# Moving the weight parts of a two-block transformer kernel by 64 bytes within the on-chip memory

## Chip, cores, metric

The kernel runs on one core of a Trainium2 chip. The metric is the device time of one execution, in microseconds (us). It runs a whole small network: a hybrid block of two layers, the second of them with a mixture of experts, and a second block of two layers with attention. All of it is in float32, for one sequence of 256 tokens of width 1024.

## The reference, cut to what matters

```python
def swiglu(h, w1, w3, w2):
    a = jnp.einsum("btd,df->btf", h, w1)
    g = jnp.einsum("btd,df->btf", h, w3)
    return jnp.einsum("btf,fd->btd", jax.nn.silu(a) * g, w2)      # d 1024, f 2816

def moe_swiglu(h, w_router, w1, w3, w2):                          # 8 experts, top 2
    ...
    for e in range(N_EXPERTS):
        out = out + combine[..., e:e + 1] * swiglu(h, w1[e], w3[e], w2[e])
    return out

def reference(...):
    x = first_block(...)     # 2 layers: mixer (h @ w_in ... @ w_out), then swiglu or moe_swiglu
    return second_block(...) # 2 layers: attention (h @ w_in ... @ w_out), then swiglu
```

Around each of these eight steps there are norms, a modulation (shift, scale and gate from a vector `c`) and a residual sum.

## The kernel before

**Exact parts.** A product of float32 numbers is made of three fast matmuls. Each operand is split into a high part and a low part, and `mm3` (lines 166 to 168) adds high times high, high times low and low times high into the same accumulator in PSUM. The activations' parts are made where the activations are made. The weights come from memory as blocks of 1 MB into a buffer `raw` (in the experts also `rawx`), and `split_now` makes two halves of each block into parts: ScalarE copies 128x1024 numbers, rounded, into a tile `hi` (line 147), and VectorE subtracts that from the block into a tile `lo` (line 148). TensorE then reads `hi` and `lo`.

**Moving and stationary.** `matmul(out, lhsT=..., rhs=...)` loads `lhsT` into the array (a row PEld in the profile) and streams `rhs` through it. A profile's group name gives the moving operand first: `pp<-h,hi` streams the activations `h` through the weights `hi`, and `pp<-hi,xe` streams the weights `hi` through the activations `xe`.

**The stages**, in order of time: a mixer (44 to 175 us), a dense feed-forward (198 to 383), the second mixer (383 to 541), the router (541 to 589), eight experts (589 to 1384), attention (1407 to 1546), feed-forward (1570 to 1753), attention (1753 to 1893), feed-forward (1915 to 2100).

- A **feed-forward** goes in 11 steps of 256 hidden columns. From the second step on, `proj_tr` streams `h` (256 columns) through the weights: 2 matrices x 2 halves x 8 x 3 = 96 matmuls. Then `down` (line 634) streams 512 columns of the weights w2 through the hidden activations, which lie in scratch tiles `s`: 24 matmuls. In the first step the roles in the projection are the other way round (`pp<-hi,h`).
- An **expert** goes in five blocks of 512 hidden columns and one of 256. Weights are moving, the gathered tokens stationary; these tokens lie in scratch tiles `xe` for experts 0, 1, 4 and 5, and in the tiles `h` and `x` for experts 2, 3, 6 and 7. The product with w2 streams weights through scratch tiles `s` into `ya`.
- **Mixer and attention** use `proj_nat` for most products: weights moving, `h` stationary, 256 wide (`pj<-hi,h`). Their output product is 512 wide, with weights moving.

**Where tiles lie.** Each pool of tiles takes one piece of every partition of the on-chip memory, the pools behind one another in the order in which they are opened. `__init__` opens const, raw, hi, lo, x, h, t, macc, gate, col; the scratch pools of each step (`xe`, `s`, `y`, `rawx` and others) are opened later and lie behind these. Tiles of raw, x and h have 8192 bytes per partition, those of hi, lo, macc and gate 4096; the 32 tiles of t take 4096 bytes in all, the ten of col 320. So in the kernel before, the start addresses in a partition are these (the same slice steps of 512 bytes and more are used inside all of them):

| tiles | first address, bytes | remainder by 256 |
|---|---|---|
| raw | 24736 | 160 |
| hi | 57504 | 160 |
| lo | 82080 | 160 |
| x | 106656 | 160 |
| h | 131232 | 160 |
| macc | 151712 | 160 |
| first scratch tiles (f, xe, sh) | 168416 | 224 |
| s of 2048 bytes, y, rawx | 172512, 214496, 209376 | 224 |

Some scratch tiles of the two mixers have the remainder 32, since a pool with tiles of 1036 bytes lies ahead of them.

Of the kernel before, what the change touches and what calls it, by code (L numbers as in the profile page):

```python
# [20 lines left out]
KD = 8  # L21
# [38 lines left out]
# the second block's attention, in units of four heads: Q queries and keys, V values, A attention, F modulation  # L60
# [3 lines left out]
class _Net:  # L64
    def __init__(self, ctx, tc, a, out):
        self.tc, self.nc, self.a, self.out = tc, tc.nc, a, out
        self.pools = {}
        self.ctx = ctx
        for name, bufs in (("const", 1), ("raw", 4), ("hi", 6), ("lo", 6), ("x", 3), ("h", 1),
                           ("t", 32), ("macc", 2), ("gate", 2), ("col", 10)):  # L70
            self.pools[name] = ctx.enter_context(tc.tile_pool(name=name, bufs=bufs))
        self.n = 0
        self.bar, self.free = None, 0
        self.step = self.nraw = 0
# [11 lines left out]
    @contextmanager  # L86
    def phase(self, **sizes):
        """Scratch pools of one part of the program."""
        saved = dict(self.pools)
        with ExitStack() as st:  # L90
            for name, bufs in sizes.items():
                kw = {"space": PSUM} if name in ("pp", "pa", "ya", "pj", "sa", "sb", "sd") else {}
                self.pools[name] = st.enter_context(self.tc.tile_pool(name=name, bufs=bufs, **kw))
            yield
        self.pools = saved
# [26 lines left out]
    @contextmanager  # L122
    def behind(self):
        """Vector work that is issued behind the last normalisation's short steps."""
        ins = self.bar
        if ins is None or not any(i is ins for i in self.nc.cur_bb.bb.instructions):
            yield
            return
        with self.tc.issue_after(ins):
            yield  # L130
# [8 lines left out]
    def split_now(self, v):  # L139
        """Exact high and low parts of a [128, k, n] block: two lists of k tiles."""  # L140
        k, n = v.shape[1], v.shape[2]
        H, L = [], []
        for z in range(0, k, k // 2):
            m = k // 2
            h = self.tl("hi", [128, 1024], F32R)[:, :m * n].rearrange("p (k n) -> p k n", k=m)
            l = self.tl("lo", [128, 1024], F32R)[:, :m * n].rearrange("p (k n) -> p k n", k=m)
            self.nc.scalar.copy(h, v[:, z:z + m])  # L147
            self.nc.vector.tensor_tensor(l, v[:, z:z + m], h.bitcast(F32), ALU.subtract)  # L148
            H += [h[:, j] for j in range(m)]
            L += [l[:, j] for j in range(m)]  # L150
        return H, L
# [7 lines left out]
    def mm3(self, out, a, b, start, stop):  # L159
        """out += a^T b, a and b given as exact (high, low) parts."""  # L160
        mm = self.nc.tensor.matmul
        if b[1] is None:
            for i in range(2):
                mm(out, lhsT=a[i].bitcast(F32), rhs=b[0], start=start and i == 0, stop=stop and i == 1)
            return
        mm(out, lhsT=a[0], rhs=b[0], start=start, stop=False)  # L166
        mm(out, lhsT=a[0], rhs=b[1], start=False, stop=False)  # L167
        mm(out, lhsT=a[1], rhs=b[0], start=False, stop=stop)  # L168
# [9 lines left out]
    def rsqrt(self, v, n):  # L178
        """1/sqrt of v (> 0) to float32 accuracy."""
# [17 lines left out]
    def evac_split(self, ps, hi, lo, A=None, B=None):  # L197
        """ps [128, 2, n] in PSUM -> exact parts of ps * A + B (columns per middle index)."""
# [30 lines left out]
    def fill(self, n):  # L229
        """n more blocks of two rows of 128 of the modulation's product, behind the rest."""  # L230
# [15 lines left out]
    def plus(self, key, out, in_):  # L246
        """A gate row: the first layers add 1 to it."""
        if key[0] < 2:
            self.nc.scalar.activation(out, in_, ACT.Identity, bias=self.ones[:, 0:1])
        else:  # L250
            self.nc.scalar.copy(out, in_)

    def mod_gate_pe(self, key):
        """A gate on every partition, straight from the tensor engine, one half of the columns after the other."""
# [19 lines left out]
    def mod_rows(self, key):  # L274
        """Two rows of 128 into the sums by partition."""
# [20 lines left out]
    def mod_done(self, key):  # L296
        """The finished vector: a gate on every partition, shift and scale (plus 1) as columns."""
# [13 lines left out]
        if self.step in (2, 6):  # L311
            # the tensor engine is the busy one there: transposes, summed by the scalar engine
# [22 lines left out]
    def setup(self):  # L335
# [26 lines left out]
        def stack(tag, names, eng):  # L362
            """Vectors of 128-multiples, all as columns of one tile."""
# [58 lines left out]
    def rows(self, ap, n):  # L422
        """A row vector of n numbers, the same on every partition."""
        t = self.sc([128, n])
        self.nc.gpsimd.dma_start(out=t, in_=ap.partition_broadcast(128))
        return t

# [8 lines left out]
    def layer_norm(self, x):  # L436
        """x normalised (no gain, no bias), mostly on the scalar engine."""
# [19 lines left out]
    def affine(self, x, g, b):  # L457
        """x * g + b in place, with rows g and b from DRAM."""
# [12 lines left out]
    def make_hf(self, xn, A, B):  # L471
        """h^T = (xn * A + B)^T, [128, KD, T]."""
# [13 lines left out]
    def make_h(self, xn, A, B):  # L486
        """h^T = (xn * A + B)^T as exact parts, [128, KD, T]."""
# [21 lines left out]
    def ab(self, l, s, g=None, b=None):  # L509
        """Columns A = g (1 + scale), B = b (1 + scale) + shift."""  # L510
# [13 lines left out]
    def resid(self, get, x, gate, ln, norm=True):  # L524
        """xr = x (ALPHA with ln) + gate * y, y from get(t, h); xr and its rows normalised."""
# [43 lines left out]
    def resid_rms(self, get, x, gate, gb):  # L569
        """As resid with a layer norm (gain and bias rows in gb), then rows normalised by their mean square."""  # L570
# [34 lines left out]
    def proj_nat(self, h, w, c0):  # L605
        """h @ w[:, c0:c0+256], tokens on partitions: PSUM [128, 2, 256]."""
# [13 lines left out]
    def down(self, accs, blocks, t=None):  # L620
        """accs[t][h] += y^T W over blocks of 128 rows: (y parts, W parts, start, stop)."""
# [15 lines left out]
    def proj_out(self, accs, w, parts, last):  # L637
        """accs = y w over parts of 256 rows (row block, exact parts of y^T); token tiles apart in the last ones."""
# [17 lines left out]
    def ffn(self, h, w1, w3, w2, fill):  # L656
# [10 lines left out]
        for i in range(nstep):  # L667
            pss = []
            if i == 0:
                # tokens on partitions, so that the first tile can go ahead  # L670
# [38 lines left out]
    def mixer(self, l, h, fill):  # L709
# [10 lines left out]
        # small operands  # L720
# [12 lines left out]
        # dt, latents of the attention  # L733
# [10 lines left out]
        # xs, bm, cm with channels on partitions; causal convolution and silu  # L744
# [22 lines left out]
        # softplus  # L767
# [14 lines left out]
        # a, cumulative sums, decays  # L782
# [17 lines left out]
        # x with tokens on partitions  # L800
# [18 lines left out]
        # C B^T within the chunks  # L819
# [8 lines left out]
        for c in range(2):  # L828
            yp = self.ps(pool="sd")
            for g in range(2):  # L830
                # exp of the summed a from s to l, 0 where l < s
# [23 lines left out]
        # latent attention  # L855
# [57 lines left out]
        # what the output product takes, all parts  # L913
# [21 lines left out]
        # spatial gating  # L935
# [39 lines left out]
        # gate of the scan, twice silu(z); then normalised  # L975
# [36 lines left out]
    def scores(self, qT, kT, pool="pa"):  # L1012
        """Masked scores of one head, [128, 384]: (q0 k0), (q1 k0), (q1 k1)."""
# [6 lines left out]
    def softmax(self, p, scale, scol, sm):  # L1020
        """exp(scale (s - max)) and its sums; scale a number or columns by token tile."""
# [24 lines left out]
    def route(self, xn, hf):  # L1046
# [37 lines left out]
        # exact parts of xn  # L1084
# [4 lines left out]
        # sums over the experts stay in PSUM  # L1089
# [14 lines left out]
    def moe_over(self, st, A, B):  # L1104
        """Ranks from 128 on, for any expert with more than 128 tokens."""
# [5 lines left out]
    def granules(self):  # L1111
        """The experts' weights in the order of their use."""
# [18 lines left out]
    def expert_in(self, base, es, pos, gate, xh, xl, A, B):  # L1131
        """One-hot slots, gathered inputs (exact parts) and gates by slot for two experts, in pieces."""
# [122 lines left out]
    def rope_setup(self):  # L1255
        """cos and sin of position * frequency for any position, by exact reduction."""
# [14 lines left out]
        def rnd(dst, src, unit):  # L1271
            """src rounded to a multiple of unit, divided by unit."""
            V.tensor_scalar(dst, src, 1.0 / unit, MAGIC, ALU.mult, ALU.add)
            V.tensor_scalar(dst, dst, MAGIC, None, ALU.subtract)
# [33 lines left out]
        # back into [-pi, pi]  # L1308
# [15 lines left out]
    def tables(self, l):  # L1324
        nc, a = self.nc, self.a
        S, V = nc.scalar, nc.vector
        # rotation tables with the gains of q and k: [128, (q k), t, 16]
# [23 lines left out]
    def attn2(self, l, h):  # L1351
# [8 lines left out]
        def project(u):  # L1360
# [19 lines left out]
            # scale of the scores by query, [128, h, t]  # L1380
            scol = self.sc([128, 4, 2])
            V.tensor_scalar(scol, rs[:, 0:8].rearrange("p (t h) -> p h t", t=2), 0.125, None, ALU.mult)
            # rotation
# [104 lines left out]
    def run(self):  # L1488
# [8 lines left out]
        # which vectors of the modulation are worked out behind each step, how far behind, and in what portions  # L1497
# [105 lines left out]
```

## Time and profile before

| | |
|---|---|
| three runs | 2097.38, 2099.36, 2099.42 us |
| median | 2099.36 us |
| span of the profiled execution | 2100.0 us |
| TensorE busy in it | 1959.5 us, 93% of the span |
| VectorE busy | 1658.0 us, 79% |
| ScalarE busy | 1208.3 us, 58% |
| read from memory | 552.19 MB, 263 GB/s over the span |

The profiled execution has no time other than its span, which is 0.6 us above the median of the runs; a sum made against the span is carried over to the median by that difference. TensorE's busy time must be read with care: matmuls overlap, each row's duration reaches from a matmul's start to its modelled end, and so a row with 283 ns can stand for matmuls that start 120 ns after each other.

### The profile page before, as it was taken

To read this page: it belongs to the slowest core of one execution; us is meant where nothing else is said; L and a number is where in the kernel's file an instruction comes from. 1 tells how busy PE (TensorE), PEld (TensorE's weight loads), DVE (VectorE), ACT (ScalarE), POOL (GpSimd) and SP (SyncE) were. 2 spreads that over 40 slices of the span, in tenths; PEclk is the share of its full clock that TensorE was granted. 3 is DMA by queue.
4 is the path that set the end of the run, shared out by engine and by line. 5 is a ranking of instruction groups with operands and counts; after the bars stand their busy time and mean duration, and the time that the engine had idled before them with its cause. 6 is when DMAs were issued, how large, how long until landed. Compare 5 with 4: busy or idle time off the path is not lost.

```text
span 2100.0 us, 30041 instructions
## 1 busy us (share of the span) xinstructions
PE 1959.5 (93%) x11481; PEld 1681.4 (80%) x11481; DVE 1658.0 (79%) x2512; ACT 1208.3 (58%) x1817; POOL 50.1 (2%) x98
## 2 busy tenths in 40 slices
PE   3998999898599999999999999969989999998999
PEld 3887999886478787878778887858869998978998
DVE  6888977897588888888888888889778877667554
ACT  3454444452378767767776777755454446545442
POOL 4000000100000000000000000000000000000000
PEclk9999999998599999999999999979999999999999
DMA  9585998565489999899989999958339894326662
GB/s 319 181 287 202 339 331 308 177 224 204 141 300 360 328 339 334 317 358 346 340 322 348 344 360 351 360 181 278 124 132 346 322 320 147 121 87 214 203 199 80
DMA packets 283238, 555.25 MB, mean 264 GB/s; under 512 B 10172, under 2 KB 137520, under 8 KB 283088
## 3 DMA queue, kind: packets, MB, share of 16 engines
q1 hardware_dynamic: 280000, 549.49, 74.6%
q0 software_dynamic: 2656, 3.20, 0.8%
q8 instruction: 91, 1.49, 0.3%
q10 hardware_dynamic: 432, 0.58, 0.1%
q14 instruction: 59, 0.48, 0.1%
HBM read 552.19 MB, written 1.05 MB: 263 GB/s over the span
## 4 chain that ended last, share of the span: by engine, by line
PE 64%; DVE 5%; ACT 2%; issue 1%; DMA 1%; ACTq 0%; DVEq 0%
PE pp L167 12%; PE pp L168 11%; PE pp L166 11%; PE pa L634 6%; PE ya L167 4%; PE ya L166 4%; PE ya L168 4%; PE pp L175 3%; PE pj L166 1%; PE pj L167 1%; PE pj L168 1%; PE pp L171 1%; DVE lo L148 1%; PE sa L171 1%; ACT hi L147 1%
## 5 line engine op out<-in xcount | busy, mean ns | idle before, releaser
L148 DVE TENSOR_TENSOR lo<-raw,hi 128x1024 fp32r<-128x1024 f32 x660 | 787.5, 1220 | 193.1 <-ACT hi L147 191.5
L147 ACT CAST hi<-raw 128x1024 fp32r<-128x1024 f32 x660 | 668.4, 1051 | 393.6 <-PE pp L167 157.9
L166 PE MATMUL pp<-h,hi 128*128 128x256 f32 x960 | 274.4, 286 | 0.0
L168 PE MATMUL pp<-h,lo 128*128 128x256 f32 x960 | 271.6, 283 | 0.0
L167 PE MATMUL pp<-h,hi 128*128 128x256 f32 x960 | 271.5, 283 | 0.0
L148 DVE TENSOR_TENSOR lo<-rawx,hi 128x1024 fp32r<-128x1024 f32 x176 | 208.5, 1220 | 42.4 <-ACT hi L147 42.3
L294 DVE SCALAR_TENSOR_TENSOR macc<-raw,const,macc 128x1024 f32<-128x1024 f32 x168 | 215.3, 1281 | 6.6 <-DMA raw<-in_ada_w_dram 2.3
L167 PEld LDWEIGHTS pp<-h,hi 128*128 128x128 f32 x960 | 184.1, 192 | 1.9 <-issue 1.2
L166 PEld LDWEIGHTS pp<-h,hi 128*128 128x128 f32 x960 | 184.0, 192 | 1.8 <-ACT hi L147 1.0
L168 PEld LDWEIGHTS pp<-h,lo 128*128 128x128 f32 x960 | 184.1, 192 | 0.0
L147 ACT CAST hi<-rawx 128x1024 fp32r<-128x1024 f32 x176 | 176.5, 1048 | 11.9 <-PE pp L168 9.9
L166 PE MATMUL pj<-hi,h 128*128 128x256 f32 x576 | 169.6, 295 | 8.2 <-ACT h L505 3.7
L167 PE MATMUL pp<-lo,h 128*128 128x512 f32 (+1 forms) x480 | 174.6, 364 | 1.2 <-DVE lo L148 1.0
L166 PE MATMUL pp<-hi,h 128*128 128x512 f32 (+1 forms) x480 | 173.0, 361 | 0.0
L167 PE MATMUL pj<-lo,h 128*128 128x256 f32 x576 | 166.0, 290 | 0.8 <-DVE lo L148 0.8
L168 PE MATMUL pj<-hi,h 128*128 128x256 f32 x576 | 165.9, 290 | 0.0
L634 PE MATMUL pa<-hi,s 128*128 128x512 f32 x528 | 151.5, 396 | 0.0
L167 PE MATMUL pp<-lo,xe 128*128 128x512 f32 (+1 forms) x384 | 146.5, 382 | 1.3 <-DVE lo L148 1.0
L166 PE MATMUL pp<-hi,xe 128*128 128x512 f32 (+1 forms) x384 | 145.2, 379 | 0.0
L168 PE MATMUL pp<-hi,xe 128*128 128x512 f32 (+1 forms) x384 | 144.7, 377 | 0.0
L168 PE MATMUL pp<-hi,x 128*128 128x512 f32 (+1 forms) x384 | 143.2, 373 | 0.0
L167 PE MATMUL ya<-lo,s 128*128 128x512 f32 x352 | 141.9, 403 | 0.0
(481 smaller groups left out, 3563.3 us busy)
## 6 DMA issues: line engine op xcount, KB each, us to landing
raw<-in_moe_w_dram SPq DMA_DIRECT2D x176, 1024.0 KB, 6.1
rawx<-in_moe_w_dram SPq DMA_DIRECT2D x88, 1024.0 KB, 6.5
raw<-in_ada_w_dram SPq DMA_DIRECT2D x48, 1024.0 KB, 6.9
raw<-in_w_mod_dram SPq DMA_DIRECT2D x48, 1024.0 KB, 6.3
raw<-in_w_in_dram SPq DMA_DIRECT2D x42, 1024.0 KB, 5.8
raw<-in_ffn_w_dram SPq DMA_DIRECT2D x33, 1024.0 KB, 6.1
raw<-in_w_gate_dram SPq DMA_DIRECT2D x22, 1024.0 KB, 5.4
raw<-in_w_up_dram SPq DMA_DIRECT2D x22, 1024.0 KB, 5.5
```

Of the source, the lines that this page charges most:

```text
L147: self.nc.scalar.copy(h, v[:, z:z + m])
L148: self.nc.vector.tensor_tensor(l, v[:, z:z + m], h.bitcast(F32), ALU.subtract)
L166: mm(out, lhsT=a[0], rhs=b[0], start=start, stop=False)
L167: mm(out, lhsT=a[0], rhs=b[1], start=False, stop=False)
L168: mm(out, lhsT=a[1], rhs=b[0], start=False, stop=stop)
L171: self.nc.tensor.matmul(out, lhsT=lhsT, rhs=rhs, start=start, stop=stop)
L175: self.nc.tensor.transpose(out, in_, self.ident[:p, :p])
L294: V.scalar_tensor_tensor(acc, v[:, i], c, acc, ALU.mult, ALU.add)
L634: mm(accs[t][h], lhsT=y[ia][:, s], rhs=W[ib][:, h * 512:(h + 1) * 512], start=start and ia == 0 and ib == 0, stop=stop and ia == 1)
```

## The change

One tile of 64 bytes per partition is placed ahead of the pool hi, and one of 192 bytes ahead of the pool x. GpSimd fills both with zeros at the start. Nothing reads them. All tiles of hi and lo so move up by 64 bytes, and all tiles of x and of the pools behind x by 256 bytes.

```diff
         self.ctx = ctx
+        self.pads = []
         for name, bufs in (("const", 1), ("raw", 4), ("hi", 6), ("lo", 6), ("x", 3), ("h", 1),
                            ("t", 32), ("macc", 2), ("gate", 2), ("col", 10)):
+            if name in ("hi", "x"):
+
+                pad = ctx.enter_context(tc.tile_pool(name=f"pad{name}", bufs=1))
+                n = 16 if name == "hi" else 48
+                self.pads.append(pad.tile([128, n], F32, name=f"pad{name}", tag="pad"))
             self.pools[name] = ctx.enter_context(tc.tile_pool(name=name, bufs=bufs))
+        for p in self.pads:
+            tc.nc.gpsimd.memset(p, 0.0)
```

The other lines of the diff drop comments and docstrings; a line number after the change is 8 higher. By the remainder by 256, the tiles stand like this:

| tiles | before | after |
|---|---|---|
| raw | 160 | 160 |
| hi, lo (the weights' parts) | 160 | 224 |
| x, h, macc | 160 | 160 |
| xe, s, y, rawx (scratch) | 224 | 224 |

The order of the instructions and what each waits for is the same on TensorE, VectorE, ScalarE and SyncE. GpSimd has two more, at the start of its program. Before, from its first row on (the names are constants and the first mixer's tiles):

```order
5 L1599 UNCONDITIONAL_BRANCH
6 L353 MEMSET const_105 128x128
7 L355 MEMSET const_107 128x128
8 L402 MEMSET const_274 128x384
9 L753 MEMSET cx_573 128x3
```

And with the change:

```order
5 L1607 UNCONDITIONAL_BRANCH
6 L79 MEMSET padhi 128x16
7 L79 MEMSET padx 128x48
8 L361 MEMSET const_115 128x128
9 L363 MEMSET const_117 128x128
10 L410 MEMSET const_284 128x384
11 L761 MEMSET cx_583 128x3
```

The two rows of the pads now stand ahead of the constants, and all that follows on GpSimd is two short instructions later.

## Rows read from the trace of the kernel before

**Rows 1.** Head of the page: the profiled execution.
```profile
span 2100.0 us, 30041 instructions
```

**Rows 2.** Windows by stage; the columns stand in the first line.
```profile
core 0: us, PE busy (x) PEld busy (x) DVE busy (x) ACT busy (x) POOL busy (x), PEclk, DMA share, GB/s
...
383.00:541.00 158.00, 128.99 (x813) 112.39 (x812) 140.34 (x293) 70.66 (x147) 10.58 (x21) 0.86 0.63 214
...
589.00:1384.00 795.00, 784.21 (x3686) 634.16 (x3684) 679.54 (x664) 578.42 (x671) 2.68 (x5) 1.00 0.96 342
...
1570.00:1753.00 183.00, 182.15 (x1261) 168.47 (x1261) 139.84 (x137) 86.03 (x153) 5.43 (x8) 1.00 0.86 305
...
1915.00:2100.00 185.00, 179.28 (x1235) 165.78 (x1233) 96.96 (x95) 73.37 (x81) 0.00 (x0) 1.00 0.53 177
...
600.00:690.00 90.00, 90.00 (x437) 74.07 (x436) 83.00 (x83) 72.66 (x84) 0.00 (x0) 1.00 0.99 359
```

**Rows 3.** Chain that ended last, 1915 to 2100 us: start, us, what.
```profile
1928.30 5.60 PE pa L634 x24
1945.40 5.60 PE pa L634 x24
```

**Rows 4.** PE groups by form, whole run; last figure ahead of the bar: mean ns.
```profile
L167 PE MATMUL pp<-h,hi 128*128 128x256 f32 x960 | 271.5, 283 | 0.0
...
L168 PE MATMUL pj<-hi,h 128*128 128x256 f32 x576 | 165.9, 290 | 0.0
L634 PE MATMUL pa<-hi,s 128*128 128x512 f32 x528 | 151.5, 396 | 0.0
...
L168 PE MATMUL ya<-hi,s 128*128 128x512 f32 x352 | 139.3, 396 | 0.0
...
L634 PE MATMUL pa<-lo,s 128*128 128x512 f32 x264 | 85.0, 396 | 0.0
```

**Rows 5.** PE groups by form, experts only, 600 to 1380 us.
```profile
L166 PE MATMUL pp<-hi,h 128*128 128x512 f32 x320 | 125.5, 393 | 0.0
L168 PE MATMUL pp<-hi,x 128*128 128x512 f32 x320 | 125.2, 391 | 0.0
...
L166 PE MATMUL pp<-hi,xe 128*128 128x512 f32 x291 | 115.4, 397 | 0.0
L168 PE MATMUL pp<-hi,xe 128*128 128x512 f32 x292 | 115.3, 395 | 0.0
...
L168 PE MATMUL pp<-hi,x 128*128 128x256 f32 x64 | 18.1, 283 | 0.0
L166 PE MATMUL pp<-hi,h 128*128 128x256 f32 x64 | 18.1, 283 | 0.0
...
L166 PE MATMUL pp<-hi,xe 128*128 128x256 f32 x64 | 17.7, 277 | 0.0
L168 PE MATMUL pp<-hi,xe 128*128 128x256 f32 x64 | 17.7, 276 | 0.0
L171 PE MATMUL pa<-s,s 128*128 128x512 f32 x56 | 17.1, 400 | 0.2
L171 PE MATMUL pp<-s,x 128*128 128x256 f32 x48 | 11.8, 279 | 0.0
```

**Rows 6.** DVE and ACT groups by form, experts only, 600 to 1380 us.
```profile
L148 DVE TENSOR_TENSOR lo<-raw,hi 128x1024 fp32r<-128x1024 f32 x339 | 398.2, 1219 | 45.6 <-ACT hi L147 44.8 <-PE pp L168 0.2
L148 DVE TENSOR_TENSOR lo<-rawx,hi 128x1024 fp32r<-128x1024 f32 x172 | 203.6, 1219 | 37.0 <-ACT hi L147 36.9
...
L147 ACT CAST hi<-raw 128x1024 fp32r<-128x1024 f32 x338 | 334.9, 1051 | 13.8 <-PE pp L168 7.6 <-PE ya L168 6.1
L147 ACT CAST hi<-rawx 128x1024 fp32r<-128x1024 f32 x171 | 171.3, 1048 | 8.6 <-PE pp L168 6.6 <-PE ya L168 2.0
```

**Rows 7.** Timeline of POOL at the start: start, us, what.
```profile
0.74 0.20 POOL L353 MEMSET const<- 128x128 f32 x1 [0.29 <-POOLq L1590]
```

**Rows 8.** Waits in the first 50 us: total, times, longest.
```profile
PE pp L171 <- DVE macc L294: 10.4, 2, 10.2
```

## The prediction

> **What bounds the kernel now.** I read the windows by stage first, to see which engine fills each stage [rows 2]. In the last feed-forward TensorE is busy 179.3 of 185 us, VectorE 97.0, ScalarE 73.4, and the transfers take a share of 0.53. In the feed-forward from 1570 us on it is 182.2 of 183, with VectorE at 139.8 and transfers at 0.86. In the experts it is 784.2 of 795, with VectorE at 679.5 and transfers at 0.96. The second mixer is different: VectorE has 140.3 of 158 us and TensorE 129.0, so there a faster matmul is at most half of the answer. TensorE's busy share includes overlapped ends, so I looked at the chain of waits next, to see whether matmuls really follow each other without a wait [rows 3]. It gives 24 matmuls of `down` in 5.60 us, 233 ns from start to start, and the same piece again 17.10 us later; the 11.50 us between hold the 96 matmuls of the next step, 120 ns each. So a step of the feed-forward is matmuls alone, and what a matmul takes is what the step takes. The experts and the two feed-forwards shown are 1163 us of the 2100.0, and the first feed-forward, of the same code, adds 185 [rows 1, 2].
>
> Last I read the groups by form, for one question: do matmuls of the same code and shape take different times when only their operands lie elsewhere? The experts are a ready experiment. Lines 166 to 168 run the same products for experts 0, 1, 4, 5 with the tokens in `xe` and for 2, 3, 6, 7 with the tokens in `h` and `x`. 256 wide, the mean is 283 ns with `h` or `x` and 276 to 277 ns with `xe`. 512 wide it is the other way round: 391 to 393 ns with `h` or `x`, 395 to 397 ns with `xe` [rows 5]. The weights lie at remainder 160 by 256 in both; `h` and `x` also at 160, `xe` at 224. I take it that the distance between the stationary operand (loaded for the next matmul while this one streams) and the moving one is what counts: distance 0 costs 6.5 ns at 256 columns, distance 64 costs 4 ns at 512. All the feed-forward's projections now stand at distance 0 and show 283 ns, and `down`, with scratch at 224, shows 396 ns [rows 4]: both fit.
>
> A rule of the Trainium skill speaks against this reading. The Trainium skill, "TensorE: Matmul & The Clock Gate", section "Step-by-step: what each phase is for", says that TensorE has two independent read ports, so that loading the next weights takes nothing from the running matmul. By that rule the change moves no time, and the kernel stays at 2099.4 us. By the rows, two equal streams of code differ by 6.5 ns; the rows decide, and the rule's case is the first rival below.
>
> **The change, part by part.** It removes nothing, and adds two memsets on GpSimd. The memset of 128x128 numbers takes 0.20 us [rows 7], so the two smaller ones take at most 0.4 us together. Behind them stand GpSimd's setup transfers, whose data TensorE takes after a product that waits 10.2 us for VectorE [rows 8]; that wait hides them. Without it they would cost 0.4 us. I take 0.
>
> The rest is the new distances (stationary less moving, by 256):
>
> - **Feed-forward projections**, from step 2 on: `h` moving at 160, weights stationary at 224; distance 0 becomes 64, which is `xe`'s case at 256 columns. 3 x 960 matmuls [rows 4] x -6.5 ns (283 to 276.5) = **-18.7 us**. All of it is on the path.
> - **`down` of the feed-forward**: moving and stationary both at 224; 64 becomes 0. 528 + 264 matmuls [rows 4] x -4 ns (396 to 392) = **-3.2 us**.
> - **Experts, 512 wide with scratch tiles** (`ya<-hi,s`, 3 x 352 [rows 4], and `xe`, some 875 [rows 5]): 64 becomes 0. 1931 x -4 ns = **-7.7 us**.
> - **Experts, 512 wide with `h` and `x`** (3 x 320 [rows 5]): 0 becomes -64, the weights now ahead. No row has this at 512 columns. Bounds: nothing, and +4 ns as at distance 64 (393 to 397). I take the loss: 960 x 4 = **+3.8 us**.
> - **Experts, 256 wide**: with `xe` 64 becomes 0, 192 x +6.5 = +1.2 us. With `h` and `x` 0 becomes -64. The row nearest to that is the gather `pp<-s,x` (scratch moving, `x` stationary): 279 against 283 [rows 5], so -4 ns x 192 = -0.8 us. Together **+0.4 us**.
> - **`proj_nat`** in mixers and attention (`pj<-hi,h`, 3 x 576 [rows 4]) and in the first step of the three feed-forwards (3 x 96 by the code): 0 becomes -64, again -4 ns by the gather's row. 2016 x 4 = 8.1 us. Its cover is VectorE's work, as the mixer's window shows [rows 2]. Bounds: 0 and -8.1. I take half, **-4.0 us**.
> - **`proj_tr` of the mixers** (2 x 144 by the code): -6.5 ns each, 1.9 us, of which half, **-0.9 us**.
> - **The splits** (lines 147 and 148): block at 160, parts now at 224. The row for it is `rawx`, 64 away the other way round: 1219 ns with `raw` and with `rawx` on VectorE, 1051 and 1048 ns on ScalarE [rows 6]. I take **0**; what a loss would do is the fourth rival.
>
> Sum: -18.7 - 3.2 - 7.7 + 3.8 + 0.4 - 4.0 - 0.9 = -30.3 us. The span of 2100.0 [rows 1] becomes 2069.7 us; it lies 0.6 us above the median of the runs shown, so I forecast **2069 us**, 1.4% less.
>
> What is late next: a feed-forward step goes from 17.10 to about 16.4 us. In the feed-forward at 1570 us the transfers must then rise from 305 to 318 GB/s, and VectorE from 76% to 80% of its time; the experts showed 359 GB/s over 90 us [rows 2]. In the experts TensorE wins only 3.5 us of 795, so transfers at 342 GB/s need hardly more.
>
> **The rivals.**
> 1. *The change does nothing.* What separates `xe` from `h` may be where they lie in the large (37 thousand bytes apart), not the remainder. Then pads of 64 and 192 bytes change no time: **2099 us**. For it: no row has the same operands at another remainder. Against it: two widths react with opposite signs, which fits two streams that meet at other points better than a slow region. Chance 0.13. The rule of the Trainium skill above gives the same time.
> 2. *Transfers hold the middle stages.* If 0.86 and 0.96 are already all that the memory gives at these sizes, only the last feed-forward (a third of 21.9) and the half of the small products gain: -7.3 - 4.9 = -12.2, **2087 us**. Against it stand the 0.99 and 359 GB/s from 600 to 690 us [rows 2]. Chance 0.07.
> 3. *Equal remainders help only at 160.* `pa<-s,s`, both operands at 224, shows 400 ns, not 392 [rows 5]. It has few matmuls and waits of its own, so it weighs little; but if it holds, `down`, `ya` and `xe` win nothing, and the sum is -30.3 + 3.2 + 7.7 = -19.4: **2080 us**. Chance 0.15.
> 4. *Slower: the splits.* If a block at 160 with parts at 224 slows VectorE's subtraction, the experts feel it first: 511 splits there [rows 6] and 795 - 679.5 = 115 us free [rows 2], so a split may grow by 0.23 us, to 1.45, before VectorE sets the pace. Above that each 0.1 us costs 51 us there. The feed-forwards and the rest still give back 27 us, so the kernel is slower from about 1.50 us a split; at 1.6 us VectorE needs 874 us in the experts, 79 more than now, and the time is about **2150 us**. The equal rows for `raw` and `rawx` speak against it. Chance 0.08.
>
> **How the numbers follow.** The forecast has 0.57. Its own range: all of `proj_nat` and `proj_tr` on the path (-4.9 more), no loss with `h` and `x` (-3.8), and 1 ns more on the 512-wide (-2.7) give 2058; none of the small products and half of the 512-wide gain give 2079. Rivals 3 and 2 lie above, to 2087. With 3 us for its bounds, the range **2058 to 2090** holds the forecast and rivals 2 and 3, 0.79. Faster by over 0.2% (4 us, about what a measurement of this kernel can tell from no change) is the same three cases, **0.79**; no change is rival 1, **0.13**; slower is rival 4, **0.08**.
>
> **What would show it.** Right: `pp<-h,hi` 256 wide falls from 283 to about 276.5 ns, `pa<-hi,s` and `ya<-hi,s` from 396 to about 392, `pp<-hi,xe` 256 wide rises to 283, and the piece of 24 `down` in the chain returns after about 16.4 instead of 17.10 us. The three feed-forwards shorten by about 7 us each. Wrong: 283 ns unchanged (rival 1); shorter matmuls with waits of ScalarE on transfers between them (rival 2); line 148 above 1219 ns (rival 4). A 512-wide row that rises with both operands at 224 breaks the idea that distance alone counts.

## The result and the profile after

The changed kernel took 2076.23 us (median of 4 runs, 2074.29 to 2077.88) against 2099.14 us for the kernel before, a ratio of 0.9893 with a 95% interval from 0.9879 to 0.9907. In a later comparison it stood at 0.9896 (0.9882 to 0.991). The profiled execution has a span of 2074.9 us, 25.1 less than before [rows 1].

The windows by stage of the profile after, in the columns of [rows 2]; boundaries are moved with the stages:

```profile
core 0: us, PE busy (x) PEld busy (x) DVE busy (x) ACT busy (x) POOL busy (x), PEclk, DMA share, GB/s
...
376.00:534.00 158.00, 128.33 (x815) 111.42 (x814) 140.59 (x295) 70.87 (x147) 10.59 (x21) 0.87 0.62 214
582.00:1375.00 793.00, 778.72 (x3684) 633.94 (x3685) 681.99 (x670) 581.55 (x673) 2.68 (x5) 1.00 0.95 343
...
1556.00:1731.00 175.00, 175.00 (x1258) 162.91 (x1257) 137.91 (x135) 83.86 (x152) 5.17 (x8) 1.00 0.91 319
...
1894.00:2074.00 180.00, 175.16 (x1238) 163.34 (x1236) 96.86 (x95) 73.80 (x82) 0.00 (x0) 1.00 0.53 182
```

The feed-forwards have shrunk, the experts a little, the mixer not at all. Measured between the starts of the same matmuls in both traces (the first matmul at or after each boundary of the kernel before, and its counterpart), the first feed-forward went from 184.90 to 178.39 us, the one in the middle from 182.24 to 175.79, and the last one lost 4.51 us: 17.5 us together. The experts went from 798.16 to 793.13 us, 5.0 less. Mixers and attention, in order of time, changed by -0.02, -0.24, -0.42 and +0.34 us. The other 2.3 us are the first 44 us, the router and the norms, which differ between two executions of one kernel too: in the second profiled execution of the changed kernel (span 2078.6 us) they come to less than 1 us. There the experts (-5.0) and the last feed-forward (-4.5) stand as they were, the other two feed-forwards gained 0.4 us less each (-6.1 and -6.0), and the first attention took 1.8 us more than before.

The groups of TensorE by form, whole run, after; the first three answer to [rows 4], the others to [rows 5], which were taken in the experts alone:

```profile
L175 PE MATMUL pp<-h,hi 128*128 128x256 f32 x960 | 267.3, 278 | 0.0
...
L642 PE MATMUL pa<-hi,s 128*128 128x512 f32 x528 | 148.2, 389 | 0.0
...
L176 PE MATMUL ya<-hi,s 128*128 128x512 f32 x352 | 137.7, 391 | 0.0
...
L174 PE MATMUL pp<-hi,h 128*128 128x512 f32 x320 | 126.0, 394 | 0.0
L176 PE MATMUL pp<-hi,x 128*128 128x512 f32 x320 | 125.6, 393 | 0.0
L174 PE MATMUL pp<-hi,xe 128*128 128x512 f32 x320 | 125.5, 393 | 0.0
L176 PE MATMUL pp<-hi,xe 128*128 128x512 f32 x320 | 125.0, 391 | 0.0
...
L176 PE MATMUL pp<-hi,xe 128*128 128x256 f32 x64 | 18.1, 283 | 0.0
L174 PE MATMUL pp<-hi,xe 128*128 128x256 f32 x64 | 18.1, 282 | 0.0
L176 PE MATMUL pp<-hi,x 128*128 128x256 f32 x64 | 17.9, 280 | 0.0
```

Every row whose new distance the rows before had shown moved to the value seen there. `xe` at 256 columns, now at distance 0, has the 283 and 282 ns that `h` and `x` had; `down` and `ya`, now at 0, fell to 389 and 391; the feed-forward's projections fell from 283, but to 278 and not to 276.5. The splits did not move: 1220 ns on VectorE with `raw` and with `rawx`, 1049 on ScalarE. These are their rows in the experts, as in [rows 6]:

```profile
L156 DVE TENSOR_TENSOR lo<-raw,hi 128x1024 fp32r<-128x1024 f32 x338 | 396.8, 1220 | 43.3 <-ACT hi L155 42.4
L156 DVE TENSOR_TENSOR lo<-rawx,hi 128x1024 fp32r<-128x1024 f32 x169 | 199.9, 1220 | 36.2 <-ACT hi L155 35.1
...
L155 ACT CAST hi<-raw 128x1024 fp32r<-128x1024 f32 x336 | 332.2, 1049 | 11.7 <-PE pp L176 6.8 <-PE ya L176 4.3 <-DVE lo L156 0.3
```

Why 278, the chain shows. This is the feed-forward that starts at 1556 us, after (start, us, what):

```profile
1572.73 1.72 PE pp L179 x4
1574.44 0.12 PE pp L174
1585.34 5.45 PE pa L642 x24
1602.10 5.44 PE pa L642 x24
1607.55 0.87 PE pp L183 x8
1608.42 0.12 PE pp L174
1619.31 5.47 PE pa L642 x24
```

From 1574.44 to 1585.34 there are 96 projections, 113.5 ns each; from 1608.42 to 1619.31 there are 96 more, 113.4 ns each. Both steps follow a small product of the modulation (line 179, line 183). But between the `down` that ends at 1590.79 and the next at 1602.10 lie 11.31 us, 117.8 ns for each of 96: this step follows straight on `down`. So the new distance has two paces, 113.4 and 117.8 ns, and after its first few matmuls a step keeps one of them to its last. Counted by starts, 16 of the 30 steps ran at 113.4 in this execution and 14 at 117.8, 8 of these in the last feed-forward, which has little modulation between its steps. The pace is not fixed by the program alone: in the second profiled execution two of the 16 steps, one in each of the first two feed-forwards, ran at 117.8 behind the same small product. Their second matmul started 201 ns after the first, where it was 205 or 206 ns in the first execution. Each such step costs 96 x 4.4 ns = 0.42 us, which is what these two feed-forwards gained less.

### The profile page after: what moved, and what is told of

The parts are those of the page before. It is cut to its first block, busy times and chain, and to the rows that moved or that the text cites. A ratio compares the mean times of both kernels' runs of the same rounds, so it can differ in the third digit from the quotient of the medians.

```text
span 2074.9 us, 30043 instructions
## 1 busy us (share of the span) xinstructions
PE 1931.9 (93%) x11481; PEld 1664.2 (80%) x11481; DVE 1656.2 (80%) x2512; ACT 1206.9 (58%) x1817; POOL 49.9 (2%) x100
## 4 chain that ended last, share of the span: by engine, by line
PE 61%; DVE 7%; ACT 3%; issue 2%; DMA 1%; ACTq 0%; DVEq 0%
PE pp L175 11%; PE pp L176 11%; PE pp L174 11%; PE pa L642 6%; PE ya L175 4%; PE ya L174 4%; PE ya L176 4%; PE pp L183 3%; DVE lo L156 2%; PE pp L179 1%; PE pj L174 1%; PE pj L175 1%; PE pj L176 1%; PE sa L179 1%; ACT hi L155 1%
## 5 line engine op out<-in xcount | busy, mean ns | idle before, releaser
L156 DVE TENSOR_TENSOR lo<-raw,hi 128x1024 fp32r<-128x1024 f32 x660 | 786.6, 1220 | 167.9 <-ACT hi L155 162.3
L174 PE MATMUL pp<-h,hi 128*128 128x256 f32 x960 | 270.3, 282 | 0.0
L175 PE MATMUL pp<-h,hi 128*128 128x256 f32 x960 | 267.3, 278 | 0.0
L176 PE MATMUL pp<-h,lo 128*128 128x256 f32 x960 | 267.2, 278 | 0.0
L156 DVE TENSOR_TENSOR lo<-rawx,hi 128x1024 fp32r<-128x1024 f32 x176 | 208.4, 1220 | 40.0 <-ACT hi L155 38.6
L175 PEld LDWEIGHTS pp<-h,hi 128*128 128x128 f32 x960 | 180.2, 188 | 1.7 <-issue 1.2
L174 PEld LDWEIGHTS pp<-h,hi 128*128 128x128 f32 x960 | 180.2, 188 | 1.7 <-ACT hi L155 1.2
```

## The experiments

All were compared with the kernel before. "Pace" is the mean from start to start over matmuls that follow each other without a wait. Edits are to `__init__` of the changed kernel, unless said otherwise.

**All moved alike.** One pad of 64 bytes ahead of hi, none ahead of x.

```diff
-            if name in ("hi", "x"):
+            if name in {'hi': 16}:
...
-                n = 16 if name == "hi" else 48
+                n = {'hi': 16}[name]
```

> One pad of 64 bytes ahead of the weights' parts, none ahead of x: parts, activations and scratch all move by 64 bytes, so the distances between stationary and moving operands are those of the kernel before, at other addresses. Theory 'distance' (stationary less moving, by 256 bytes, sets the pace): 2099 us, within 0.2%; 256-wide in the feed-forward back at 120 ns from start to start, down at 233 ns. Rival 'place' (a remainder of 224 is good in itself for the weights' parts): the gain of the change stays, 2076 us; 256-wide at 113 to 118 ns.

Measured: 2100.31 us, ratio 0.9997 (0.9989 to 1.0006). The groups by form:

```profile
L175 PE MATMUL pp<-h,hi 128*128 128x256 f32 x960 | 271.6, 283 | 0.0
...
L642 PE MATMUL pa<-hi,s 128*128 128x512 f32 x528 | 151.5, 396 | 0.0
```

These are the numbers of [rows 4], with the weights' parts at remainder 224 as in the changed kernel. The place by itself is worth nothing, and so is the distance of the blocks in `raw` from the parts, which is 64 here as in the changed kernel. What is left is the distance between the operands. The expert blocks 256 wide with `xe`, at distance 64 before and here, show the two paces as well: before, all four runs of 48 matmuls were at 113.4 ns, here two of them at 113.4 and two at 117.8.

**Activations moved, weights' parts left.** Pads `{'x': 16}`: parts at 160, activations at 224, scratch at 32.

> One pad of 64 bytes ahead of x, none ahead of the weights' parts: parts stay at 160, activations at 224, scratch at 32. Theory 'distance': feed-forward projections at -64 (weights behind the moving activations), as the changed kernel's mixer products: 117.7 ns instead of 120 in the kernel before, -6 us; experts fed from h and x at +64, 233 ns, +4 us; products fed from scratch at 128, which no row shows (bounds 227 and 234 ns, -17 to +2 us over 2723 matmuls). In all 2080 to 2100 us. Rival 'place': the weights' parts lie where they lay before, so no gain, 2099 us, all 256-wide at 120 ns.

Measured: 2093.07 us, ratio 0.9962 (0.9948 to 0.9976).

```profile
L175 PE MATMUL pp<-h,hi 128*128 128x256 f32 x960 | 268.2, 279 | 0.0
...
L642 PE MATMUL pa<-hi,s 128*128 128x512 f32 x528 | 151.4, 395 | 0.0
...
L174 PE MATMUL pp<-hi,h 128*128 128x512 f32 x320 | 126.8, 397 | 0.0
```

The projections have distance -64 here and a pace of 117.7 ns, the same as the changed kernel's `pj<-hi,h` at -64. The experts fed from `h` at +64 went up to 233.4 ns. The products fed from scratch, at 128, stayed at 232.8. The first two paces are those that the same distances had elsewhere, and the third lies within the bounds given; the rival's 2099 us is out. The run also bears on the period: counted by 512 bytes, the scratch tiles of the kernel before lie 320 from the parts and `h` lies 64 from them here, and both give 233.4 ns at 512 columns, which fits a count by 256 and not one by 512.

**128 bytes.** Pads `{'hi': 32, 'x': 32}`: parts at 32, activations at 160, scratch at 224.

> 128 bytes ahead of the weights' parts, 128 more ahead of x: parts at 32, activations at 160, scratch at 224. Theory 'distance': mixer and feed-forward projections at 128, which no row shows (bounds: 113 and 120 ns); products fed from scratch at -64, 229.8 ns instead of 233.4, -9 us against the kernel before. If 128 by 256 is as good as 64: 2070 to 2080 us; if the pattern repeats every 128 bytes, 128 is as bad as 0: 120 ns, and about 2090 us.

Measured: 2092.03 us, ratio 0.9958 (0.9945 to 0.9972).

```profile
L175 PE MATMUL pp<-h,hi 128*128 128x256 f32 x960 | 270.7, 282 | 0.0
...
L642 PE MATMUL pa<-hi,s 128*128 128x512 f32 x528 | 149.4, 392 | 0.0
```

At 128 the 256-wide products are at 119.1 ns in the mean (steps of the feed-forwards between 118.6 and 120.0), hardly below the 119.8 of distance 0. The 512-wide at -64 have 229.6 ns, as forecast. The time is near the 2090 us of the case "128 is as bad as 0" for 256 columns, but at 512 columns 128 is not like 0: 232.9 ns for the experts fed from `h` and `x`, against 228.4. So the pattern does not repeat every 128 bytes.

**32 bytes.** `n = 8 if name == "hi" else 56`: parts at 192, activations at 160, scratch at 224.

> Pads of 32 and 224 bytes: weights' parts at 192, activations at 160, scratch at 224, so feed-forward projections at a distance of 32, mixer products at -32, products fed from scratch at 32. If the pace changes gradually with distance: 256-wide near 117 ns, 512-wide near 231 ns, about 2088 us. If it goes by steps of 64 bytes and 32 counts as 0: 256-wide at 120 ns, 512-wide at 228 ns: -13 us, 2086 us. If 32 counts as 64: 256-wide at 113 to 118 ns, 512-wide at 233 ns: -13 us too; the pace of each width tells these apart.

Measured: 2096.5 us, ratio 0.9985 (0.9974 to 0.9995).

```profile
L175 PE MATMUL pp<-h,hi 128*128 128x256 f32 x960 | 269.7, 281 | 0.0
...
L642 PE MATMUL pa<-hi,s 128*128 128x512 f32 x528 | 151.5, 396 | 0.0
```

A miss for all three expectations: 256-wide 118.3 ns, between 0 and 64; 512-wide 233.3 ns, as at 64. The two widths do not follow one curve. Mean paces of all runs, in ns (stationary less moving, by 256 bytes):

| distance | 256 columns | 512 columns |
|---|---|---|
| 0 | 119.8 | 228.4 |
| 32 | 118.3 | 233.3 |
| 64 | 113.4 or 117.8 | 233.4 |
| 128 | 119.1 | 232.9 |
| -64 | 117.7 | 229.7 |
| -32 | 117.0 | 233.4 |

The rows 32 and -32 come from this run alone. The others were met in two layouts or more, at other addresses, and at 256 columns also with the roles of parts and activations exchanged. Apart from 64 at 256 columns, where the two paces mix, the means of one distance lie within 1 ns of each other; single groups differ more (at 0 and 512 columns, `down` has 227.0 ns and `ya` 229.1).

**Scratch back at 64.** The changed kernel with a third pad of 64 bytes between col and the scratch pools.

```diff
+        pad = ctx.enter_context(tc.tile_pool(name="padscr", bufs=1))
+        self.pads.append(pad.tile([128, 16], F32, name="padscr", tag="pad"))
         for p in self.pads:
             tc.nc.gpsimd.memset(p, 0.0)
```

> The changed kernel with a third pad of 64 bytes ahead of the scratch pools, so that scratch stands 64 from the weights' parts again, as in the kernel before, and only the activations keep their new distance. Theory 'distance', parts added up: the 2723 products 512 wide that are fed from scratch go back from 228.3 to 233.4 ns, +13.5 us (5 in the feed-forwards, 8 in the experts), the 256-wide with xe give 1 us back: 2076 + 12.5 = 2089 us. Rival: their gain was hidden in the experts, where transfers are at 0.96: only +5 us, 2081 us.

Measured: 2087.53 us, ratio 0.9941 (0.9928 to 0.9953).

```profile
L177 PE MATMUL pp<-h,hi 128*128 128x256 f32 x960 | 267.5, 279 | 0.0
...
L644 PE MATMUL pa<-hi,s 128*128 128x512 f32 x528 | 151.3, 395 | 0.0
L178 PE MATMUL ya<-hi,s 128*128 128x512 f32 x352 | 139.2, 395 | 0.0
```

The products fed from scratch are back at 233.4 ns, the projections keep their gain, and the experts take 799.35 us where the changed kernel takes 793.13. So the change is two gains that add up, and the experts' part was not held by transfers.

This run also shows the two paces side by side. In its last feed-forward, steps that follow straight on `down` are fast and slow by turns (chain: start, us, what):

```profile
1933.92 5.60 PE pa L644 x24
1950.42 5.59 PE pa L644 x24
1967.32 5.60 PE pa L644 x24
```

From `down` to `down` it is 16.50 us, then 16.90. Of the 14 steps that follow straight on `down`, 6 ran at 113.4 to 113.5 ns, and each began 235 or 236 ns after the last matmul of `down`; the other 8 ran at 117.8 and began 228 to 230 ns after it. In the changed kernel all 14 began 226 or 227 ns after it, and all were slow.

**A tiny matmul ahead of every step.** In `ffn`, steps 2 to 11; its result is overwritten by the projection that follows.

```diff
                     p = self.ps((128, 2, T))
+                    if w is w1:
+                        self.mm(p[:, 0, 0:1], self.zero, self.zero[:, 0:1])
```

> The changed kernel with one tiny bfloat16 matmul (1 column, overwritten afterwards) ahead of the first projection of steps 2 to 11 of each feed-forward: 30 more matmuls. In the changed kernel 15 of the 30 steps run at 117.8 ns a matmul, those that follow straight on down; the others, which follow another product, at 113.4. Theory 'entry' (what precedes a run sets how its two operand streams stand, and the run keeps it): all 30 steps at 113.4 ns; 15 x 96 x 4.4 ns = -6.3 us, less 30 x about 0.1 us, so -3 us, 2073 us. Rival: the two paces come from something else (fill work of VectorE or transfers, or which buffers are used), so 15 slow steps stay, and the kernel is 1 to 3 us slower than the changed one, 2078 us.

Measured: 2074.29 us, ratio 0.9875 (0.9859 to 0.9891). 24 steps ran at 113.4 to 113.5 ns and 6 at 117.8. All 14 steps that had been slow became fast (the expectation counted 15); the 6 slow ones had been fast before and follow another small product, with the tiny one now in between. One such matmul at the entry of a run is enough to switch its pace, both ways, with the same work of VectorE, the same transfers and the same buffers around it; the rival is refuted. This is the entry of one of the 6 slow steps:

```profile
1892.62 0.17 PE L179 MATMUL pp<-const 128*128 128x1 bf16 x1
1892.65 0.36 PE L174 MATMUL pp<-h,hi 128*128 128x256 f32 x1
1892.85 0.28 PE L175 MATMUL pp<-h,hi 128*128 128x256 f32 x1
```

**The tiny matmul only where a step follows straight on `down`.**

```diff
-                    if w is w1:
+                    if w is w1 and i in {2: (3, 6, 8), 6: (3, 6, 9), 8: (2, 3, 4, 5, 6, 8, 9, 10)}[self.step]:
```

> The changed kernel with the tiny matmul only ahead of the 14 feed-forward steps that follow straight on down (3, 3 and 8 in the three feed-forwards), which ran at 117.8 ns. Theory 'entry': all 30 steps at 113.4 to 113.5 ns; each of the 14 wins 96 x 4.3 ns and pays 0.24 us, so -0.17 us a step, -2.4 us in all, the last feed-forward alone -1.4 us: 2074 us. Rival: steps elsewhere fall back to 117.8 ns and nothing is won, 2076 to 2079 us.

> The changed kernel itself once more, beside the others of this call. Both theories: 2076 us, 0.989 of the kernel before.

Measured side by side: 2074.23 us, ratio 0.9882 (0.9868 to 0.9896), with the tiny matmuls, and 2078.72 us, 0.9896 (0.9882 to 0.991), without. All 30 steps ran at 113.4 to 113.5 ns. One step of the last feed-forward without the tiny matmul (the changed kernel's chain, then its timeline) and one with it (timeline, then chain):

```profile
1940.58 5.44 PE pa L642 x24
1957.33 5.44 PE pa L642 x24
```

```profile
1929.11 0.28 PE L174 MATMUL pp<-h,hi 128*128 128x256 f32 x1
1929.23 0.28 PE L175 MATMUL pp<-h,hi 128*128 128x256 f32 x1
```

```profile
1927.02 0.18 PE L179 MATMUL pp<-const 128*128 128x1 bf16 x1
1927.06 0.36 PE L174 MATMUL pp<-h,hi 128*128 128x256 f32 x1
1927.26 0.28 PE L175 MATMUL pp<-h,hi 128*128 128x256 f32 x1
...
1938.04 0.63 PE L642 MATMUL pa<-hi,s 128*128 128x512 f32 x2
```

```profile
1921.73 5.45 PE pa L642 x24
1938.20 5.45 PE pa L642 x24
```

Without it the second matmul starts 0.12 us after the first; with it, 0.20 us after, and from there 95 starts fill 1927.26 to 1938.04, 113.5 ns each. The 0.20 us are not themselves what makes a step fast: the slow step shown above has them too. A step takes 16.47 us from `down` to `down` instead of 16.75. That is 0.28 us less a step, more than the 0.17 forecast: the 96 matmuls win 0.41 us, so the tiny matmul cost about 0.13 us and not the 0.24 expected. Over the last feed-forward, from the first `down` of the chain to the last one, it is 149.90 against 152.06 us. The medians point the same way, but their intervals overlap: the steps are shown to be faster, the whole kernel only probably.

## Why the prediction was right, and where it was off

The forecast was 2069 us and the range 2058 to 2090; the result lies in it, 7 us above the forecast. The mechanism, distance between stationary and moving operand, is shown by the run in which all moved alike and by the one in which only the activations moved. That the time came within 7 us is partly luck: two terms were too good, by 6.3 and about 5 us, and two others too bad, by 1.7 and 2.8. Term by term, with what matched pairs of matmuls of both traces show:

- **Feed-forward projections**, -18.7 us forecast: mis-sized. They gave -12.4 us over 2834 pairs. The step that failed is "`xe`'s case at 256 columns", -6.5 ns for each: in the experts of the kernel before, all these runs were at the pace of 113.4, and in the feed-forward 14 of 30 steps were at 117.8. So 16 steps won about 6.4 ns a matmul and 14 about 2.0, and the piece of 24 `down` returned after 16.75 us in the last feed-forward, not after 16.4. The rows before could not show the second pace: only two of the four `xe` runs were at 113.4 when all tiles had moved alike. The two runs with the tiny matmul show that the entry of the run decides.
- **`down`**, -3.2 forecast: -4.9 us over 754 pairs, 6.5 ns each instead of 4. The 4 ns were read from group means of the experts; from start to start the same rows differ by 4.9 (233.4 against 228.5), and `down` at distance 0 reached 227.0, below every group of the experts.
- **Experts, 512 wide with scratch**, -7.7 forecast: -8.2 us (the forecast counted 875 matmuls with `xe` of 960, since its window began at 600 us and the experts at 589). **With `h` and `x`**, +3.8 forecast: +1.0 us, 1.1 ns each; this was the unshown case, and its true price lay near the lower bound. **256 wide**, +0.4 forecast: +0.75 us. Forecast together at -3.5 us, the pairs give about -6.4, and the stage became 5.0 us shorter.
- **Mixers and attention**, -4.9 forecast for the half on the path: nothing that stands out. Their matmuls did get faster (1743 pairs at -64, the first steps of the feed-forwards among them, by 1.8 to 2.3 ns, not 4; 274 at 64 by 4.6 to 6.2 ns; 5.1 us in all), but the four stages together changed by -0.3 us in one profiled execution and by +0.9 in the other. Half on the path was too much. How much is covered is not shown more closely, since one of these stages alone differs by up to 2.2 us between the two executions.
- **Splits and memsets**, 0 forecast: 1220 and 1049 ns, as before. The rival that VectorE slows is refuted. The first mixer began 0.4 us earlier than before, so the memsets cost nothing that shows.
- **Transfers** did not hold the feed-forwards: the middle one moved 319 GB/s (305 before) and became 6.45 us shorter, as the first did (6.51). The rival is refuted, and by the run with scratch at 64 for the experts too.
- **"Equal remainders help only at 160"** is refuted: `down` and `ya` fell at 224. `pa<-s,s`, which raised the doubt, still shows 404 ns with both operands at one remainder; why that small group is slower is not settled.
- **The rule of the Trainium skill**, "TensorE: Matmul & The Clock Gate", section "Step-by-step: what each phase is for", says that the weight load takes nothing from the running matmul. Taken as the forecast that the change moves no time, it is refuted by the measured 22.9 us: the same code gains or loses up to 6.5 ns a matmul with the distance alone. That it is the two reads that get in each other's way is an inference; no trace here shows the reads.

What stays open is where and how the two operands affect each other. The table of paces was measured, not derived; nothing here shows why 64 and -64 differ, why the widths differ, or why an entry fixes the pace.

## What to carry to other kernels

Where a stage is a dense run of matmuls, compare groups of the same shape whose operands lie in different pools: a difference of some ns between them is a sign that the distance of the stationary from the moving operand, by 256 bytes, is worth a pad. The two operand pairs of one kernel can want different distances, so one pad for the weights and one ahead of the scratch are two separate knobs, and each is to be measured at its own width. Read the pace from start to start, since group means hide it, and look whether whole runs take one of two values.

## What was not expected of the hardware

- A run of 256-wide matmuls at distance 64 has two steady paces, 113.4 and 117.8 ns, and keeps the one it enters with for all 96 matmuls. One matmul of a single column ahead of the run switches it, and without one the steps straight behind `down` were fast when they began 235 or 236 ns after its last matmul and slow at 226 to 230 ns.
- The best distance depends on the width: in the mean, 0 is the slowest of six at 256 columns (119.8 ns) and the fastest at 512 (228.4 ns).
- The sign matters: at 256 columns 64 gives 113.4 or 117.8 ns, while -64 gives 117.7, and none of the 30 feed-forward steps of the run at -64 reached 113.4; at 512 columns 64 gives 233.4 and -64 gives 229.7 ns.
